# Value pages of paged attention in twelve segments of four or six, instead of sixteen rounds of four

## The chip, the cores and the metric

The kernel runs on one core of one Trainium2 chip. The metric is the device time of one execution in microseconds (us). A core has a matrix engine (TensorE, in the profile PE for matmuls and PEld for the loading of its stationary operand), a vector engine (VectorE, DVE), a scalar engine (ScalarE, ACT), a general engine (GpSimd, POOL) and SyncE (SP), which here only issues DMAs. Each engine runs its own instruction stream in order, and waits on semaphores for the others.

## What is computed

One layer of a decoder runs over 288 tokens: 256 of a prompt, and 32 new ones (8 sequences of 4 tokens) that attend to a paged cache of 1024 earlier rows each. The layer is a feed-forward block, a mixing block, a second feed-forward block, a gated embedding, and a last norm. The change touches one product in the mixing block, the probabilities of the 32 new tokens times the cached values:

```python
def fox_sample(q, k_new, v_new, logf_new, cache_k, cache_v, cache_logf, page_table):
    ...
    v_past = cache_v[page_table].reshape(DB, P, N_HEADS, HEAD_DIM)
    ...
    v_all = jnp.concatenate([v_past.astype(k_new.dtype), v_new], axis=1)
    ...
    p = jax.nn.softmax(s, axis=-1)
    return jnp.einsum('bhqk,bkhd->bqhd', p.astype(v_all.dtype), v_all)
```

There are 8 sequences, 8 pages for each, 128 rows in a page, 8 heads of 128 columns: 64 value pages of 128 x 1024 fp32, 512 KB each. All else in the layer is products of the 288 tokens with weights that are read once.

## The kernel before

**Weight products.** All tokens stand transposed, features on the 128 partitions and 288 tokens along the free axis. A helper, `pair` (L313), makes 256 output features at a time, in chunks of four blocks of 128 input features. For one chunk it needs one weight tile `wraw` of 512 KB, which ScalarE and VectorE split into a high and a low part (`whi`, `wlo`, L294). A chunk is 24 matmuls: for each of 2 output halves and 4 blocks, two with the high weights (L340) and one with the low ones (L342), each streaming 288 columns.

**Order.** The work is a list `steps`. The mixing block's list is written by hand: `fill` is a row of chunks numbered from 0, and `at(i, f)` sets a step `f` ahead of chunk `i`. `between` merges both. A scheduler then lays out every engine's stream, following this order as a priority where the data allow it.

**Loads.** Each step names the items it needs, weights (kind "w") and value pages (kind "p"). `load_upto` (L243) runs ahead of the step by `AHEAD` = 12 items. Weights are issued by SP into four slots in this stage; pages by POOL, as an indirect DMA that gathers 128 rows by index (L261). A page takes one of seven places (`page_tile`, L266): three weight slots that are lent out, three tiles of the pool `vx`, and the tile `wideb`, which holds the scores of the second group of sequences until they have been turned and is first given to page 12. So up to page 11 there are six places. A load can be issued only after the last matmul that read the place's page before.

**The value product.** The 8 sequences are two groups `gi` of four. `probs_t` (L800) turns the probabilities of a group; a sequence's 32 columns (8 heads x 4 tokens) are the stationary operand, 128 x 32, and half a page, 128 x 512, streams past. The matrix engine is cut into four column tiles of 32 columns for it: sequence `b` of the group uses column tile `b`, and its output is 32 rows of a PSUM bank. Two banks `va` hold a group's sums: bank `e` belongs to half `e` of the page's columns (heads 4e to 4e+3). `v_round` (L819) adds page `r` of all four sequences: for e = 0, 1 and b = 0 to 3 one matmul into bank `e`, column tile `b`. Fp32 operands make each a pair of matmul instructions in the trace, so a round has 16. There are 8 rounds for each group, set 2.7 chunks apart (`VSTEP`), ahead of chunks 51, 53, 56, 59, 61, 64, 67, 69 and 72, 75, 78, 80, 82, 86, 88, 91.

**The end of a group.** After its last round `sample_out` (L836) adds the four new tokens (L841, 32 x 32 tiles), picks each row's own head out of the eight blocks with a mask (8 VectorE instructions), and later `sample_turn` (L853) transposes the result (L856) and copies it into `oS` (L858, two copies).

**Other work between the rounds.** Steps `prompt_head` stand 2.5 chunks apart from chunk 69 on. POOL also builds their masks (L878, L879), sums squares (L923, L980) and, from chunk 80 on, adds products to the residual `h` (L1052).

Of the kernel before, what the change touches and what calls it, by code (L numbers as in the profile page):

```python
# [25 lines left out]
P = 128  # L26
# [4 lines left out]
DT = 4  # L31
NS = DB * DT
# [4 lines left out]
PAGES = 8  # L37
# [17 lines left out]
AHEAD = 12  # L55
WARM = (NT, NT, NT)
VSTEP = 2.7

GAINS = ("norm_mix", "norm_ffn2", "norm_ple", "norm_final", "norm_conv_out", "norm_attn_out", "conv_w")
A_ROWS = dict(norm_mix=D, norm_ffn2=D, norm_ple=D, norm_final=D, norm_conv_out=CB * P, norm_attn_out=NH * P,  # L60
# [36 lines left out]
def build(nc, tc, ctx, A, O):  # L97
# [3 lines left out]
    v, s, g, pe, sy = nc.vector, nc.scalar, nc.gpsimd, nc.tensor, nc.sync  # L101
# [13 lines left out]
    def bank(tag, bufs):  # L115
        return ps.tile([P, 512], F32, name=tag, tag=tag, bufs=bufs)
# [6 lines left out]
    def ktbank():  # L123

        names = [n for n in spare["tags"] for _ in range(BANKS[n])]
        spare["at"] += 1
        n = names[spare["at"] % len(names)]
        return bank(n, BANKS[n])
# [6 lines left out]
    def const(name):  # L135
        r, a, b = CONST_COLS[name]
        return C[:r, a:b]
# [7 lines left out]
    at = 0  # L145
# [4 lines left out]
    def gain(name, k):  # L150
        if name == "norm_ffn1":
            return hx[:, k:k + 1]
        a = G[name] + k
        return gT[:, a:a + 1]
# [52 lines left out]
    def split(hi, lo, x, gcol):  # L207
        return (s.activation(hi, x, AF.Copy, scale=gcol),
                v.scalar_tensor_tensor(lo, x, gcol, hi.bitcast(F32), ALU.mult, ALU.subtract))
# [100 lines left out]
    def page(src, j):  # L310
        return dict(kind="p", src=src, rows=idx[:, j:j + 1])
# [65 lines left out]
    def defer(fn, chunks=1):  # L377

        deferred.append((state["chunk"] + chunks, fn))
# [163 lines left out]
    M = {}  # L543
# [256 lines left out]
    def probs_t(gi):  # L800
        pt = wide(*(("vv", "c"), ("mix", "a"))[gi], f"PT{gi}")
        x = M["s", gi]
        for j in range(2):
            t = ktbank()
            for i in range(4):
                c = (4 * j + i) * P
                pe.transpose(t[:, i * P:i * P + P], x[:, c:c + P], ident)
            for b in range(4):
                v.tensor_copy(pt[:, j * 512:j * 512 + 512].rearrange("s (i b c x) -> s b i c x", i=4, b=4, c=4)[:, b],
                              t.rearrange("s (i c b x) -> s b i c x", i=4, c=4, b=4)[:, b])  # L810
        t = ktbank()
        pe.transpose(t[:NS, :P], x[:, PAGES * P:], ident)
        for e in range(2):
            for b in range(4):
                v.tensor_copy(pt[NS * e:NS * e + NS, 8 * P + 32 * b:8 * P + 32 * b + 32].rearrange("s (c x) -> s c x", x=8),
                              t[:NS, :P].rearrange("s (c b x) -> s b c x", c=4, b=4)[:, b])
        M["PT", gi] = pt

    def v_round(gi, r):  # L819
        its = [page(A["cache_v"], (4 * gi + b) * PAGES + r) for b in range(4)]  # L820

        def fn():
            if r == 0:
                M["va", gi] = [bank("va", BANKS["va"]) for _ in range(2)]
                M["pv", gi] = M["PT", gi].rearrange("s (r b x) -> s r b x", b=4, x=32)
            for e in range(2):
                for b in range(4):
                    pe.matmul(M["va", gi][e][32 * b:32 * b + 32, :], M["pv", gi][:, r, b],  # L828
                              its[b]["tile"][:, e * 512:e * 512 + 512], start=r == 0, stop=False, tile_position=(0, 32 * b))
            if r == PAGES - 1:  # L830
                if gi == 1:
                    state.update(through=True, wslot=WEIGHTS - 1)
                sample_out(gi)
        return (its, fn)

    def sample_out(gi):  # L836
        mx = W["vv"][0]
        for b in range(4):
            for e in range(2):
                rows = slice(NS * e, NS * e + NS)  # L840
                pe.matmul(M["va", gi][e][32 * b:32 * b + 32, :], M["pv", gi][rows, 8, b], M["vs"][rows], start=False, stop=True,  # L841
                          tile_position=(NS * e, 32 * b))
        o = mx.tile([P, P], F32, name="so", tag="so", bufs=2)
        for hh in range(NH):
            src = M["va", gi][hh // 4][:, hh % 4 * P:hh % 4 * P + P]
            m = const("headmask")[:, hh:hh + 1]
            if hh == 0:
                v.tensor_scalar(o, src, m, None, ALU.mult)
            else:
                v.scalar_tensor_tensor(o, src, m, o, ALU.mult, ALU.add)  # L850
        defer(lambda: sample_turn(gi, o), 4 if gi == 0 else 2)

    def sample_turn(gi, o):  # L853
        mx = W["vv"][0]
        t = ktbank()
        pe.transpose(t[:, :P], o, ident)  # L856
        for half in range(2):
            v.tensor_copy(M["oS"][:, 4 * half:4 * half + 4, 16 * gi:16 * gi + 16].rearrange("p c (b t) -> p c b t", t=DT),  # L858
                          t[:, :P].rearrange("p (b c a t) -> p a c b t", c=4, a=2, t=DT)[:, half])
        if gi == 1:  # L860
            s.dma_start(O["v_prompt"].rearrange("(j p) c -> p j c", p=P), M["vn"])
            for e in range(2):
                s.dma_start(O["v_sample"][:, 512 * e:512 * e + 512], M["vs"][NS * e:NS * e + NS])
            for hh in range(NH):
                split(za[hh][0][:, SEQ:], za[hh][1][:, SEQ:], M["oS"][:, hh, :], gain("norm_attn_out", hh))
            sq = mx.tile([P, NH, NS], F32, name="sqS")
            s.activation(sq, M["oS"], AF.Square)
            v.tensor_reduce(acc[:, SEQ:], sq.rearrange("p h n -> p n h"), AX.X, ALU.add)
# [173 lines left out]
    def at(i, *fns):  # L1042
        marks.setdefault(i, []).extend(fns)
# [40 lines left out]
    at(48, v_start)  # L1084
    at(50, lambda: probs_t(0))
    at(52, lambda: probs_t(1))
    for r in range(2 * PAGES):
        at({12: 82}.get(r, int(51 + VSTEP * r)), v_round(r // PAGES, r % PAGES))
    for hh in range(NH):
        at(int(69 + 2.5 * hh), lambda hh=hh: prompt_head(hh))  # L1090
    at(80, lambda: norm_scale(rsc, acc2, CB * P, 2))
# [160 lines left out]
```

## Time and profile before

| | |
|---|---|
| median of 3 executions | 2258.11 us |
| lowest and highest | 2255.43, 2260.86 us |
| the profiled execution: its own time | 2257.17 us |
| its span, from the first to the last instruction | 2255.4 us |
| mean granted TensorE clock | 0.998 |
| value rounds (L828) | from 1069.0 us on, the last at 1243.5 us |

The views of this profile are: the page (busy time per engine, the span in 40 slices, DMA queues, the chain of work that ended last, the costliest groups), the timeline (instructions in order of time, alike neighbours merged as "xN"), the instructions of one source line, the waits (who waited for whom), the chain in order of time, and busy times by stretch. All times in them are us from the span's start, unless ns is named. "mm<-x,whi" is an instruction that writes the tile `mm` and reads the tiles `x` and `whi`. A number in square brackets is idle time of that engine just before, and what ended it. A matmul's recorded length is longer than the time until the next one can start, since matmuls are pipelined; what one costs is read from the distance of starts.

### The profile page before, as it was taken

The page shows a single profiled execution, that of the slowest core. Times are in us where ns is not written, and L with a number is a line of the kernel's source. Part 1 is how long each engine was busy: PE and PEld are TensorE (multiplying, and loading weights), DVE is VectorE, ACT ScalarE, POOL GpSimd, SP SyncE. Part 2 cuts the span into 40 slices and gives each one's busy share as a digit, 9 for nine tenths or more (in the row PEclk, how much of TensorE's full clock was granted, in tenths as well). Part 3 has the DMA queues.
Part 4 walks back from the last instruction along what each step waited for, and adds up shares of the span by engine and source line. Part 5 has one row for each costly group of instructions (what it writes and reads, how often), then busy time and mean ns, then how long its engine had stood idle before and what let it go on. Part 6 is the DMA issues. An engine that isn't in the chain of part 4 may idle for free.

```text
span 2255.4 us, 44318 instructions
## 1 busy us (share of the span) xinstructions
PE 2240.5 (99%) x17387; PEld 2184.1 (97%) x17387; DVE 1341.1 (59%) x2413; ACT 1046.4 (46%) x1860; POOL 323.0 (14%) x398
## 2 busy tenths in 40 slices
PE   9999999999999999999999999999999999999997
PEld 9999999999999999888888999999999999999997
DVE  7555555555555586456466875555555555555865
ACT  6444444444444553344344554444444444444654
POOL 1020000000000013344446210000000000000210
PEclk9999999999999999999999999999999999999999
DMA  7575555555555556888988455545555555555552
GB/s 263 170 252 169 170 175 169 171 169 172 173 169 169 169 170 235 335 309 296 330 319 300 171 171 162 182 160 181 174 169 169 172 171 173 168 170 173 170 174 101
DMA packets 342849, 443.37 MB, mean 197 GB/s; under 512 B 17408, under 2 KB 307088, under 8 KB 342640
## 3 DMA queue, kind: packets, MB, share of 16 engines
q1 hardware_dynamic: 320928, 366.25, 49.5%
q0 software_dynamic: 20480, 71.67, 8.8%
q8 instruction: 136, 2.23, 0.4%
q10 hardware_dynamic: 1232, 2.62, 0.3%
q14 instruction: 73, 0.60, 0.1%
HBM read 435.41 MB, written 5.07 MB: 195 GB/s over the span
## 4 chain that ended last, share of the span: by engine, by line
PE 98%; DMA 1%; DVE 0%; issue 0%; ACT 0%; SPq 0%; DVEq 0%; POOL 0%; ACTq 0%
PE mm L340 61%; PE mm L342 31%; PE va L340 1%; PE va L828 1%; PE va L761 1%; PE va L342 1%; DMA KT<-in_cache_k_dram,idx 0%; PE kt L340 0%; DMA page<-in_cache_v_dram,idx 0%; DVE h L1178 0%; DMA h<-in_x_dram 0%; PE kt L342 0%; PE kt L882 0%; PE kt L915 0%; PE kt L906 0%
## 5 line engine op out<-in xcount | busy, mean ns | idle before, releaser
L340 PE MATMUL mm<-x,whi 128*128 128x288 f32 x7360 | 1430.5, 291 | 0.0
L294 DVE TENSOR_TENSOR wlo<-wraw,whi 128x512 fp32r<-128x512 f32 (+1 forms) x1388 | 974.3, 705 | 740.3 <-ACT whi L294 689.5
L294 ACT ACTIVATE whi<-wraw 128x512 fp32r<-128x512 f32 (+1 forms) x1388 | 861.1, 628 | 870.5 <-PE mm L340 755.6
L340 PEld LDWEIGHTS mm<-x,whi 128*128 128x128 f32 x7360 | 1163.4, 187 | 15.9 <-issue 11.0
L342 PE MATMUL mm<-x,wlo 128*128 128x288 f32 x3680 | 1067.4, 290 | 0.1
L342 PEld LDWEIGHTS mm<-x,wlo 128*128 128x128 f32 x3680 | 690.8, 188 | 0.3 <-DVE wlo L294 0.3
L340 PE MATMUL mm<-hid,whi 128*128 128x288 f32 x2816 | 544.8, 290 | 0.0
L340 PEld LDWEIGHTS mm<-hid,whi 128*128 128x128 f32 x2816 | 445.2, 187 | 0.0
L342 PE MATMUL mm<-hid,wlo 128*128 128x288 f32 x1408 | 408.3, 290 | 0.0
L412 POOL TENSOR_TENSOR sr<-sg,rs 128x288 f32<-128x288 f32 x88 | 71.5, 813 | 1385.7 <-ACT sg L410 1385.5
L342 PEld LDWEIGHTS mm<-hid,wlo 128*128 128x128 f32 x1408 | 264.3, 188 | 0.0
L432 DVE SCALAR_TENSOR_TENSOR h<-mm,h 128x288 f32<-128x288 f32 x192 | 85.5, 454 | 19.4 <-PE mm L342 19.4
L410 ACT ACTIVATE sg<-tg 128x288 f32<-128x288 f32 x88 | 39.1, 445 | 97.5 <-DVE tg L408 97.4
L738 POOL DMA_INDIRECT KT<-in_cache_k_dram,idx x64 | 65.2, 1018 | 129.1 <-DVE idx L168 51.6
L419 ACT ACTIVATE hid<-hd 128x288 fp32r<-128x288 f32 x88 | 39.2, 445 | 93.3 <-DVE hd L417 93.3
L261 POOL DMA_INDIRECT page<-in_cache_v_dram,idx x64 | 65.8, 1028 | 66.4 <-PE va L828 43.7
L234 POOL TENSOR_TENSOR acc<-acc,sq 128x288 f32<-128x288 f32 x52 | 43.8, 842 | 219.8 <-ACT sq L233 217.4
L420 DVE TENSOR_TENSOR hid<-hd,hid 128x288 fp32r<-128x288 f32 x88 | 40.1, 457 | 21.9 <-ACT hid L419 21.9
L340 PE MATMUL va<-x,whi 128*128 128x288 f32 x256 | 51.4, 295 | 0.8 <-ACT whi L294 0.8
L340 PE MATMUL mm<-zc,whi 128*128 128x288 f32 x256 | 52.0, 297 | 0.0
L417 DVE TENSOR_TENSOR hd<-mm,sr 128x288 f32<-128x288 f32 x86 | 39.0, 454 | 16.7 <-PE mm L342 16.7
L408 DVE TENSOR_TENSOR tg<-mm,rs 128x288 f32<-128x288 f32 x84 | 37.9, 451 | 14.2 <-PE mm L342 13.1
(236 smaller groups left out, 1060.0 us busy)
## 6 DMA issues: line engine op xcount, KB each, us to landing
wraw<-in_w_ffn_up_dram SPq DMA_DIRECT2D x173, 512.0 KB
wraw<-in_w_ffn_gate_dram SPq DMA_DIRECT2D x172, 512.0 KB
wraw<-in_w_ffn_down_dram SPq DMA_DIRECT2D x160, 512.0 KB
wraw<-in_w_in_dram SPq DMA_DIRECT2D x96, 512.0 KB
wraw<-in_w_out_dram SPq DMA_DIRECT2D x32, 512.0 KB
wraw<-in_w_ple_gate_dram SPq DMA_DIRECT2D x32, 512.0 KB
wraw<-in_w_ffn_down_dram SPq DMA_DIRECT2D x32, 256.0 KB
wraw<-in_w_ple_proj_dram SPq DMA_DIRECT2D x8, 256.0 KB
```

What stands on the lines that cost most here:

```text
L234: (v if k >= KT - last_on_v else g).tensor_tensor(acc, acc, sq, ALU.add)
L261: g.indirect_dma_start(out=t, out_offset=None, in_=it["src"], in_offset=bass.IndirectOffsetOnAxis(ap=it["rows"], axis=0))
L294: for i in s.activation(hi, x, AF.Copy), v.tensor_tensor(lo, x, hi.bitcast(F32), ALU.subtract):
L340: pe.matmul(o, hi[:, j % 2, w], x, start=f, stop=False)
L342: state["product"] = pe.matmul(o, lo[:, j % 2, w], xh, start=False, stop=l)
L410: s.activation(u, t, AF.Silu)
L412: g.tensor_tensor(r, u, rs, ALU.mult)
L417: v.tensor_tensor(t, o, sg[b], ALU.mult)
L419: s.activation(H["hi"][:, k, :], t, AF.Copy)
L420: v.tensor_tensor(H["lo"][:, k, :], t, H["hi"][:, k, :].bitcast(F32), ALU.subtract)
L432: v.scalar_tensor_tensor(h[:, k, :], o, 0.5, h[:, k, :], ALU.mult, ALU.add)
L738: d = g.indirect_dma_start(out=t[:, i].rearrange("p h s -> p (h s)"), out_offset=None, in_=A["cache_k"], in_offset=bass.IndirectOffsetOnAx ...
```

## The change

The list of rounds becomes a list of segments, each given by the pages that it sums. Pages are counted by row first and sequence second, so page number n of a group is row n // 4 of sequence n % 4. A group's 32 pages are cut at `VENDS`: 4, 4, 6, 6, 6, 6 for the first, 6, 6, 6, 6, 4, 4 for the second. A segment stands where the round of its last page would stand by the old rule: ahead of chunks 51, 53, 57, 61, 65, 69 and 73, 78, 82, 86, 88, 91.

In a segment the first four pages are taken as in a round: four matmuls for half 0, four for half 1. Two pages that are left over follow, both for half 0 and then both for half 1. The column tile of half 1 is moved on by two: sequence b uses tile b for half 0 and tile (b + 2) % 4 for half 1. For half 1 of the first four pages, the order of the pages is turned by two, so that the column tiles still come in the same order. `sample_out` uses the same tiles. As the rows of bank 1 now stand two sequences further on, `sample_turn` copies half 1 in two pieces.

The number of matmuls, their shapes, the pages and the weights loaded, the places for pages and `AHEAD` stay as they were.

```diff
+VENDS = ((4, 8, 14, 20, 26, 32), (6, 12, 18, 24, 28, 32))
...
-    def v_round(gi, r):
-        its = [page(A["cache_v"], (4 * gi + b) * PAGES + r) for b in range(4)]
+    def v_round(gi, pages):
+        its = [page(A["cache_v"], (4 * gi + n % 4) * PAGES + n // 4) for n in pages]
...
-            if r == 0:
+            if pages[0] == 0:
...
-            for e in range(2):
-                for b in range(4):
-                    pe.matmul(M["va", gi][e][32 * b:32 * b + 32, :], M["pv", gi][:, r, b],
-                              its[b]["tile"][:, e * 512:e * 512 + 512], start=r == 0, stop=False, tile_position=(0, 32 * b))
-            if r == PAGES - 1:
+            whole = [(i, e) for e in range(2) for i in (range(4) if e == 0 else (2, 3, 0, 1))]
+            for i, e in whole + [(i, e) for e in range(2) for i in range(4, len(pages))]:
+                r, b = divmod(pages[i], 4)
+                c = 32 * ((b + 2 * e) % 4)
+                pe.matmul(M["va", gi][e][c:c + 32, :], M["pv", gi][:, r, b], its[i]["tile"][:, e * 512:e * 512 + 512],
+                          start=r == 0, stop=False, tile_position=(0, c))
+            if pages[-1] == 4 * PAGES - 1:
...
-                pe.matmul(M["va", gi][e][32 * b:32 * b + 32, :], M["pv", gi][rows, 8, b], M["vs"][rows], start=False, stop=True,
-                          tile_position=(NS * e, 32 * b))
+                c = 32 * ((b + 2 * e) % 4)
+                pe.matmul(M["va", gi][e][c:c + 32, :], M["pv", gi][rows, 8, b], M["vs"][rows], start=False, stop=True,
+                          tile_position=(NS * e, c))
...
-        for half in range(2):
-            v.tensor_copy(M["oS"][:, 4 * half:4 * half + 4, 16 * gi:16 * gi + 16].rearrange("p c (b t) -> p c b t", t=DT),
-                          t[:, :P].rearrange("p (b c a t) -> p a c b t", c=4, a=2, t=DT)[:, half])
+        for half, to, at, n in (0, 0, 0, 4), (1, 0, 2, 2), (1, 2, 0, 2):
+            v.tensor_copy(M["oS"][:, 4 * half:4 * half + 4, 16 * gi:16 * gi + 16].rearrange("p c (b t) -> p c b t", t=DT)[:, :, to:to + n],
+                          t[:, :P].rearrange("p (b c a t) -> p a c b t", c=4, a=2, t=DT)[:, half][:, :, at:at + n])
...
-    for r in range(2 * PAGES):
-        at({12: 82}.get(r, int(51 + VSTEP * r)), v_round(r // PAGES, r % PAGES))
+    for gi, ends in enumerate(VENDS):
+        for a, b in zip((0,) + ends, ends):
+            at(int(51 + VSTEP * ((32 * gi + b) / 4 - 1)), v_round(gi, range(a, b)))
```

## The prediction, made before the changed kernel ran

> **What bounds the kernel now.** First the page: busy time, the slices, the chain that ended last.
>
> ```profile
> span 2255.4 us, 44318 instructions
> PE 2240.5 (99%) x17387; PEld 2184.1 (97%) x17387; DVE 1341.1 (59%) x2413; ACT 1046.4 (46%) x1860; POOL 323.0 (14%) x398
> DMA  7575555555555556888988455545555555555552
> PE 98%; DMA 1%; DVE 0%; issue 0%; ACT 0%; SPq 0%; DVEq 0%; POOL 0%; ACTq 0%
> ```
>
> PE is the chain: 98% of it. Whatever the change brings must come out of PE's own stream, or out of a wait of PE. The DMA row says where a wait could come from: in slices 17 to 22 (some 900 to 1240 us) the DMA engines are busy 8 to 9 tenths, elsewhere about 5. The value rounds lie there. The profiled execution took 2257.17 us, 1.8 us more than its span and 0.9 us less than the median of 2258.11; I sum against 2257.17.
>
> Next the timeline of PE around the first round, to price a round.
>
> ```profile
> 1068.74 0.29 PE L342 MATMUL mm<-x,wlo 128*128 128x288 f32 x1
> 1068.96 1.92 PE L828 MATMUL va<-page,PT 128*32 128x512 f32 x16
> 1070.82 0.54 PE L340 MATMUL mm<-x,whi 128*128 128x288 f32 x2
> ...
> 1071.98 0.29 PE L342 MATMUL mm<-x,wlo 128*128 128x288 f32 x1
> ...
> 1073.14 0.29 PE L342 MATMUL mm<-x,wlo 128*128 128x288 f32 x1
> ```
>
> From 1071.98 to 1073.14 nine weight matmuls start, 0.129 us each: the undisturbed pace. From 1068.74 to 1071.98 there are also nine, but it takes 3.24 us. 3.24 - 9 x 0.129 = **2.08 us** is what a round costs PE. How much of it is matmul work shows when a round is cut by the edge of a window:
>
> ```profile
> 1144.04 1.50 PE L828 MATMUL va<-page,PT 128*32 128x512 f32 x12
> ```
>
> ```profile
> 1144.04 1.93 PE L828 MATMUL va<-page,PT 128*32 128x512 f32 x16
> 1145.89 1.09 PE L841 MATMUL va<-vs,PT 32*32 32x512 f32 x16
> 1146.91 0.49 PE L881 MATMUL kt<-k,q 128*128 128x128 f32 x2
> ```
>
> Four more matmuls, one for each column tile, take 0.43 us. They run side by side, since the instructions of one line last this long each:
>
> ```profile
> L828 PE MATMUL va<-page,PT x256: 592/592/617, 1069.0 to 1244.9; 128*32 128x512 f32 x128
> ```
>
> A round of 16 is four such batches, 1.72 us; the other 2.08 - 1.72 = 0.36 us is going into the tiled product and out of it again (0.22 instead of 0.13 us ahead of it, and a slow first pair of weight matmuls behind).
>
> Last, where PE waited. The waits from 1066 to 1250 us and the chain in order of time agree on one place, the third round; the timeline shows its length.
>
> ```profile
> PEld va L828 <- DMA page<-in_cache_v_dram,idx: 1.0, 1, 1.0
> ```
>
> ```profile
> 1082.97 7.76 DMA page<-in_cache_v_dram,idx
> 1090.78 1.90 PE va L828 x10
> ```
>
> ```profile
> 1089.61 3.06 PE L828 MATMUL va<-page,PT 128*32 128x512 f32 x16
> ```
>
> A page issued at 1082.97 landed 7.76 us later; the round took 3.06 instead of 1.92 us, **1.14 us** lost. In all other rounds PE had its pages in time.
>
> **The change part by part.**
>
> *Fewer rounds.* 64 pages are 256 matmuls, 64 batches, before and after: eight segments of six batches and four of four. What goes is four times the way in and out: 4 x 0.36 = **1.45 us**. This holds if the two pages left over fill the array. They come as column tiles b, b+1 for half 0 and b+2, b+3 for half 1: four different tiles, so one batch for each of the two instructions of a product. Two banks are then written side by side. The row of L841 above shows that already: 16 instructions on eight tiles, alternating between the banks, in 1.02 us (1145.89 to 1146.91), about two batches. With two tiles at a time instead, eight segments would pay two batches more each, 8 x 2 x 0.43 = 6.9 us. I take no loss.
>
> *The third round's wait.* The four pages of that round are now first read one chunk later (57 for 56), 24 x 0.129 = 3.1 us, more than the 1.14 us that were short. Two more pages are read in the same segment, 4 batches (1.7 us) behind its start. POOL issues them behind the late one:
>
> ```profile
> 1082.97 0.94 POOL L261 DMA_INDIRECT page<-in_cache_v_dram,idx  x1 [0.30 <-PE mm L342]
> 1084.21 1.41 POOL L261 DMA_INDIRECT page<-in_cache_v_dram,idx  x1 [0.31 <-issue]
> 1085.92 0.94 POOL L261 DMA_INDIRECT page<-in_cache_v_dram,idx  x1 [0.30 <-PE mm L342]
> ```
>
> With 7.76 us again, those land by 1093.7; the segment would start at 1089.6 + 3.2 = 1092.8 and read them from 1094.5. So **-1.14 us**; zero if the pages issued later are slower by more.
>
> *Pages in bursts of five.* There are seven places. With rounds of four, three pages of the next round were there when a round ended. With a segment of six, one page of the next is, and five must be issued once the segment's first four pages are read, 1.85 us after its start T; POOL issues one each 1.25 us:
>
> ```profile
> 1104.94 0.94 POOL L261 DMA_INDIRECT page<-in_cache_v_dram,idx  x1 [6.99 <-PE va L828]
> 1106.19 0.94 POOL L261 DMA_INDIRECT page<-in_cache_v_dram,idx  x1 [0.30 <-issue]
> 1107.43 0.94 POOL L261 DMA_INDIRECT page<-in_cache_v_dram,idx  x1 [0.30 <-PE mm L342]
> 1108.68 0.94 POOL L261 DMA_INDIRECT page<-in_cache_v_dram,idx  x1 [0.30 <-issue]
> ```
>
> The fifth goes out at T + 6.9. With 7.76 us to landing it is there at T + 14.6. The busy times by stretch, cut at the starts of rounds, give the interval:
>
> ```profile
> 1111.71:1123.07 11.36, 11.36 (x90) 9.77 (x89) 4.64 (x9) 3.71 (x7) 4.28 (x4) 1.00 0.97 366
> 1123.07:1135.10 12.03, 12.03 (x95) 10.41 (x95) 5.84 (x12) 3.79 (x7) 4.13 (x4) 1.00 0.89 333
> ```
>
> The first stretch is three chunks and a round: a chunk is (11.36 - 1.85) / 3 = 3.2 us. Four chunks and a segment of six (2.7 us) are 15.4 us, 16.1 with the transposes of the second stretch; the last two pages are read 1.7 us into the next segment, T + 17. That leaves 2.5 us. The first stretch also shows DMA share 0.97 at 366 GB/s, so a fifth page in a row may need longer than 7.76 us; no row has such a burst. Bounds: nothing, or 1.5 us in each of the four intervals between chunks 57 and 73; I take 0.5 us in all, near the nothing that 2.5 us of room give.
>
> The Trainium skill, in "DMA: Bandwidth & Descriptors", section on the anatomy of a DMA on the GpSimd path, fits such a load as 2.0 us and its bytes at 436 GB/s; for 512 KB that is an estimate of 3.2 us, by which neither this term nor the next would exist and the sum would be -2.6 us. The trace has 7.76 us, and I go by the trace.
>
> *The pair of segments at 86 and 88.* Two chunks apart, with six pages ahead of four: only one of the four is there, three must be issued, where before one was. POOL's timeline there:
>
> ```profile
> 1222.77 2.38 POOL L1052 TENSOR_TENSOR h<-h,tB 128x288 f32<-128x288 f32 x2 [1.00 <-DVE tB L1051]
> 1225.30 0.95 POOL L261 DMA_INDIRECT page<-in_cache_v_dram,idx  x1 [0.15 <-issue]
> 1226.56 0.94 POOL L261 DMA_INDIRECT page<-in_cache_v_dram,idx  x1 [0.30 <-PE mm L340]
> 1227.80 1.11 POOL L261 DMA_INDIRECT page<-in_cache_v_dram,idx  x1 [0.31 <-PE mm L342]
> ```
>
> ```profile
> 1221.24 1.93 PE L828 MATMUL va<-page,PT 128*32 128x512 f32 x16
> ```
>
> ```profile
> 1231.15 1.92 PE L828 MATMUL va<-page,PT 128*32 128x512 f32 x16
> ```
>
> The interval is 9.91 us and becomes 10.8 with two batches more. The page issued at 1225.30 landed within 5.85 us, as PE did not wait for it at 1231.15. The third page goes out at T + 4.4 if POOL turns to the pages at once, at 1227.80 - 1221.24 = T + 6.6 behind the two adds, and lands 5.85 to 7.76 us later: T + 10.2 to T + 14.3, against 10.8. PE loses 0 to 3.5 us; I take **1.4 us**, POOL going to the pages after one of the adds. Behind PE's wait stand only weight matmuls; their weights are loaded meanwhile.
>
> *Small parts.* Two more copies of `oS` on DVE, off the chain:
>
> ```profile
> L858 DVE COPY oS<-kt x4: 212/214/224, 1161.9 to 1251.7; 128x64 f32<-128x64 f32 x4
> ```
>
> DVE is 59% busy, so they cost nothing; without cover 0.4 us. L841 keeps eight different tiles: nothing, within one batch (0.43 us) either way for each group.
>
> **The sum:** -1.45 - 1.14 + 0.5 + 1.4 = -0.7 us. 2257.17 - 0.7 = **2256.5 us**. By the bounds: from -2.6 to -1.45 + 6 + 3.5 = +8 us.
>
> **Rivals.**
>
> *Late pages, slower.* The mechanism of the bursts, at its upper end: every segment of six that follows another by four chunks starts 2 us short, because 5 pages and the weights share DMA engines that stand at 0.97. Six such intervals (chunks 57 to 73 and 78 to 86) and 3 us at 88: 15 us, less 2.6: about 2269.6; with half the waits 2262. It decides from some 10 us to landing for the fifth page. For it: 7.76 us for a third page in a row. Against: the mean rate, 10 tiles of 0.52 MB in 15.4 us, 340 GB/s, is below the 366 that a stretch moved.
>
> The Trainium skill, in "SBUF — State Buffer", section "SBUF: two separate sides", says that POOL cannot write a DMA's descriptors while VectorE holds the port they share. That would stretch bursts. The trace bears it out little: issues of L261 last 936 ns at least, 942 in the median, 2020 at most.
>
> *Left-over pages do not share the array* (the change fails to do what it says): -1.45 + 6.9 - 1.14 + 1.9 gives 2263.4. Against it stands the row of L841.
>
> *Nothing gained:* the way in and out costs a longer segment more, or the waits are worth what the rounds were: 2257 to 2258.
>
> *More gained:* no wait anywhere, 2254.6, and a favourable draw of executions.
>
> **How the numbers follow.** A measurement of this kernel can tell some 0.2%, 4.5 us. Forecast (2254.5 to 2258.5) 0.65; nothing gained 0.10; late pages 0.17; array not shared 0.03; more gained 0.05. Executions of the kernel before ranged over 5.4 us, so the range is wider than the bounds of the forecast: 2252.5 to 2263. Faster by over 0.2% needs more than the whole saving, only spread can show it: 0.07. Slower: late pages and unshared array, less their milder half, 0.16. Within: 0.77.
>
> **What would show it.** Twelve groups of L828, of 24 matmuls in about 2.78 us or of 16 in 1.92. If a group of 24 takes near 4.5 us without a DMA wait, the array is not shared. Waits of PEld at L828 for page DMAs: one of 1 to 2 us at the segment of chunk 88, none at the third segment. If such waits sum to more than 6 us, the bursts decide and the forecast is wrong. If DVE or ACT end waits of PE, the scheduler has moved other work, which I left out.

## The result: slower by 0.3%, and the profile after

| | before | changed |
|---|---|---|
| median of 7 executions, us | 2256.78 | 2264.86 |
| lowest and highest, us | 2255.43, 2260.86 | 2261.20, 2266.16 |
| the profiled execution, us | 2257.17 | 2261.20 |
| its span, us | 2255.4 | 2259.4 |

The ratio changed / before is 1.003, with a 95% interval of 1.0021 to 1.004. The changed kernel is slower, by 8 us in the medians. Its profiled execution happens to be its fastest one; a second trace, from a usual execution, comes with the experiments.

The page of the changed kernel reads almost as before: the span and the chain that ended last. The lines have moved by one to four: L831 is now the value product, L262 the page load, L341 and L343 the weight products.

```profile
span 2259.4 us, 44310 instructions
PE 98%; DVE 1%; DMA 1%; issue 0%; POOL 0%; ACT 0%; DVEq 0%; ACTq 0%; POOLq 0%
```

DVE has come up to 1%. Where the time went shows in the chain in order of time, from 1060 to 1262 us, here without its PE pieces for weights:

```profile
1067.96 1.95 PE va L831 x16
1070.08 1.04 POOL page L262
1071.43 0.98 POOL page L262
1072.71 7.39 DMA page<-in_cache_v_dram,idx
1080.15 1.90 PE va L831 x10
1095.32 2.71 PE va L831 x24
...
1195.73 0.99 DVE zc L210
...
1228.53 6.64 DMA page<-in_cache_v_dram,idx
1235.21 1.91 PE va L831 x12
```

Two page loads that PE waited for now stand on the chain, where the kernel before had one, and a stretch of DVE's work lies on the chain near 1195 us. The timeline of PE gives the lengths. The second segment (chunk 53, four pages, as before) and the one at chunk 88 (four pages):

```profile
1077.15 1.40 PE L831 MATMUL va<-page,PT 128*32 128x512 f32 x6
1080.15 1.90 PE L831 MATMUL va<-page,PT 128*32 128x512 f32 x10 [1.60 <-DMA page<-in_cache_v_dram,idx]
...
1231.59 1.04 PE L831 MATMUL va<-page,PT 128*32 128x512 f32 x2
1233.94 1.05 PE L831 MATMUL va<-page,PT 128*32 128x512 f32 x2 [1.30 <-DMA page<-in_cache_v_dram,idx]
1235.21 1.91 PE L831 MATMUL va<-page,PT 128*32 128x512 f32 x12 [0.23 <-DMA page<-in_cache_v_dram,idx]
```

The first lasts 1080.15 + 1.90 - 1077.15 = 4.90 us instead of 1.92: **3.0 us** lost at chunk 53. The other lasts 1235.21 + 1.91 - 1231.59 = 5.53: **3.6 us** lost at chunk 88. Each time some of the matmuls run, and the rest stand until a page lands.

The third segment, which in the old place waited for 1.14 us, does not wait, and a segment of six looks like this:

```profile
1095.25 2.78 PE L831 MATMUL va<-page,PT 128*32 128x512 f32 x24
```

2.78 - 1.92 = 0.86 us more than four pages, two batches, so the two left-over pages do share the array. Eight such additions are 6.9 us, four rounds less at 2.06 us (the same reading of the first round, 1068.74 to 1071.19 less three weight matmuls) are 8.2 us: **1.4 us** saved.

The last piece is at the norm of the conv group, ahead of the output projection. PE's timeline there, after and then before:

```profile
1200.52 0.40 PE L192 MATMUL kt<-sqh,meanr 128*128 128x288 f32 x1
1201.27 0.40 PE L192 MATMUL kt<-sql,meanr 128*128 128x288 f32 x1 [0.35 <-DVE sql L205]
```

```profile
1202.45 0.38 PE L191 MATMUL kt<-sqh,meanr 128*128 128x288 f32 x1
1202.67 0.29 PE L191 MATMUL kt<-sql,meanr 128*128 128x288 f32 x1
```

The second matmul comes 0.75 instead of 0.22 us behind the first: PE has reached it before VectorE has made `sql`. With a second such wait of 0.3 us in the product before (for `zc`, the last rows of the conv group), and what each adds around it, PE loses **1.1 us** that the kernel before did not lose.

The account of this execution: -1.4 - 1.1 + 3.0 + 3.6 + 1.1 = +5.2 us. The spans differ by 4.0, since the first segment of this execution also began 1.1 us earlier (1067.9 against 1069.0 us), with the same program ahead of it: the spread of executions.

### The profile page after: what moved, and what is told of

It reads as the page before. It is cut to its first block, busy times and chain, and to the rows that moved or that the text cites. A ratio compares the mean times of both kernels' runs of the same rounds, so it can differ in the third digit from the quotient of the medians.

```text
span 2259.4 us, 44310 instructions
## 1 busy us (share of the span) xinstructions
PE 2242.1 (99%) x17387; PEld 2184.8 (97%) x17387; DVE 1344.8 (60%) x2415; ACT 1047.1 (46%) x1860; POOL 321.2 (14%) x398
## 3 DMA queue, kind: packets, MB, share of 16 engines
q8 instruction: 136, 2.23, 0.4%
## 4 chain that ended last, share of the span: by engine, by line
PE 98%; DVE 1%; DMA 1%; issue 0%; POOL 0%; ACT 0%; DVEq 0%; ACTq 0%; POOLq 0%
PE mm L341 61%; PE mm L343 30%; PE va L341 2%; PE va L831 1%; PE va L762 1%; PE va L343 1%; DMA page<-in_cache_v_dram,idx 1%; PE kt L341 0%; DVE h L1183 0%; PE kt L343 0%; PE mm L521 0%; PE kt L886 0%; PE kt L919 0%; DVE wlo L295 0%; PE kt L910 0%
## 5 line engine op out<-in xcount | busy, mean ns | idle before, releaser
L341 PE MATMUL mm<-x,whi 128*128 128x288 f32 x7360 | 1430.0, 291 | 0.0
L341 PEld LDWEIGHTS mm<-x,whi 128*128 128x128 f32 x7360 | 1163.4, 187 | 13.3 <-issue 11.8
L343 PE MATMUL mm<-x,wlo 128*128 128x288 f32 x3680 | 1067.3, 290 | 0.1
L343 PEld LDWEIGHTS mm<-x,wlo 128*128 128x128 f32 x3680 | 690.7, 188 | 0.3 <-DVE wlo L295 0.3
L341 PE MATMUL mm<-hid,whi 128*128 128x288 f32 x2816 | 544.8, 290 | 0.0
L341 PEld LDWEIGHTS mm<-hid,whi 128*128 128x128 f32 x2816 | 445.1, 187 | 0.0
L343 PE MATMUL mm<-hid,wlo 128*128 128x288 f32 x1408 | 408.3, 290 | 0.0
L343 PEld LDWEIGHTS mm<-hid,wlo 128*128 128x128 f32 x1408 | 264.3, 188 | 0.0
L262 POOL DMA_INDIRECT page<-in_cache_v_dram,idx x64 | 64.3, 1005 | 72.9 <-PE va L831 49.4
L341 PE MATMUL mm<-zc,whi 128*128 128x288 f32 x256 | 52.0, 297 | 0.1
L341 PE MATMUL va<-x,whi 128*128 128x288 f32 x256 | 51.4, 295 | 0.0
```

What stands on the lines that cost most here:

```text
L262: g.indirect_dma_start(out=t, out_offset=None, in_=it["src"], in_offset=bass.IndirectOffsetOnAxis(ap=it["rows"], axis=0))
L341: pe.matmul(o, hi[:, j % 2, w], x, start=f, stop=False)
L343: state["product"] = pe.matmul(o, lo[:, j % 2, w], xh, start=False, stop=l)
```

## The experiments

Two questions were open: why does a segment wait whose four pages, places and chunk are as before, and why are the three pages at chunk 88 so late? Four kernels were run together; the kernel before had a median of 2256.94 us beside them.

**Release order.** The trace names, for each wait of PE, the semaphore of the load it waits for. In the kernel before, the second round waits for the first and second load of POOL's burst after the first round; in the changed kernel for the second and third, and the third segment waits for the first. By these waits POOL has put page 8 ahead of pages 6 and 7. Page 8 takes the place of page 2, and the turned order (2, 3, 0, 1) of the second half reads page 2 for the last time first. So the theory: the turn lets go of the wrong place first. The edit takes only the turn out:

```diff
-            whole = [(i, e) for e in range(2) for i in (range(4) if e == 0 else (2, 3, 0, 1))]
+            whole = [(i, e) for e in range(2) for i in range(4)]
```

> The changed kernel, with the first four pages of a segment taken in the order 0, 1, 2, 3 for both halves (the turn by two taken out; column tiles and segments as changed). Theory A (release order): the turned order lets go of the third page's place first, so that POOL issues page 8 ahead of pages 6 and 7, and the segment at chunk 53 waits for page 7; here the order of issue is 6, 7, 8 again, the wait of some 3 us at the second segment is under 0.5 us, and the time is about 3 us under the changed kernel's, 2259 to 2262 us; the wait at chunk 88 stays at some 3.6 us, since all three late pages are needed at once in whatever order they come. Theory B (chance): pages 4 to 7 and their places are as before, the wait at chunk 53 is the luck of one execution; no gain, 2263 to 2266 us. The matmuls themselves should cost the same, 2.94 us for a segment of six, or up to 0.9 us more for each segment if the order of column tiles matters.

Measured: 2260.70 us (2258.41 to 2263.46), ratio to the kernel before 1.0018 [1.0009, 1.0027]; 4.2 us under the changed kernel's median. The burst, in POOL's timeline, went out at the same distances, and the second segment did not wait (PE's timeline, second fence):

```profile
1071.53 1.04 POOL L262 DMA_INDIRECT page<-in_cache_v_dram,idx  x1 [4.29 <-PE va L831]
1072.88 0.98 POOL L262 DMA_INDIRECT page<-in_cache_v_dram,idx  x1 [0.30 <-issue]
1074.17 0.94 POOL L262 DMA_INDIRECT page<-in_cache_v_dram,idx  x1 [0.30 <-PE mm L343]
```

```profile
1078.59 1.92 PE L831 MATMUL va<-page,PT 128*32 128x512 f32 x16
1109.70 3.73 PE L831 MATMUL va<-page,PT 128*32 128x512 f32 x24
1231.00 1.92 PE L831 MATMUL va<-page,PT 128*32 128x512 f32 x6
1234.59 1.90 PE L831 MATMUL va<-page,PT 128*32 128x512 f32 x10 [1.68 <-DMA page<-in_cache_v_dram,idx]
```

The segment at 1078.59 waits for the first and second load again. Chunk 88 still loses 1234.59 + 1.90 - 1231.00 - 1.92 = 3.6 us. The matmuls cost the same in the natural order. One wait is new here: 3.73 - 2.78 = 0.95 us at chunk 61, the burst of five that the prediction feared.

**The turn alone.** The same question from the other side: rounds of four at the old chunks, with the moved column tiles and the turn.

```diff
-VENDS = ((4, 8, 14, 20, 26, 32), (6, 12, 18, 24, 28, 32))
+VENDS = (range(4, 33, 4), range(4, 33, 4))
...
-        for a, b in zip((0,) + ends, ends):
-            at(int(51 + VSTEP * ((32 * gi + b) / 4 - 1)), v_round(gi, range(a, b)))
+        for a, b in zip((0,) + tuple(ends), ends):
+            at({52: 82}.get(32 * gi + b, int(51 + VSTEP * ((32 * gi + b) / 4 - 1))), v_round(gi, range(a, b)))
```

> Sixteen rounds of four at the chunks of the kernel before, but with the moved column tiles and the turned order of the second half. Theory A (release order): the turn alone moves page 8 ahead of pages 6 and 7, so a wait of 1 to 3 us shows at the second round, and 1.1 us or less stays at the third: 1 to 3 us over the kernel before. Theory B (chance, or the segments): equal to the kernel before within 1 us. A round costs PE 2.08 us in both.

Measured: 2260.74 us (2259.48 to 2263.24), ratio 1.0015 [1.0006, 1.0024]: 3.8 us lost with not one segment of six. The second round, in PE's timeline:

```profile
1079.08 1.06 PE L831 MATMUL va<-page,PT 128*32 128x512 f32 x6
1082.83 3.51 PE L831 MATMUL va<-page,PT 128*32 128x512 f32 x10 [2.69 <-DMA page<-in_cache_v_dram,idx]
```

It lost 1082.83 + 3.51 - 1079.08 - 1.92 = 5.3 us, more than expected, and the third round lost nothing. Not all of the 5.3 us is waiting: the ten matmuls behind the wait took 3.51 us instead of 1.90, and the busy times by stretch show why. PEclk, the granted clock of TensorE (the third number from the end), is 0.50 there:

```profile
1083.00:1086.40 3.40, 3.40 (x11) 0.48 (x3) 0.00 (x0) 0.00 (x0) 1.18 (x2) 0.50 0.54 219
```

So 5.3 - 1.6 = 3.7 us are the wait. The last section comes back to the clock. Both sides agree: the wait at chunk 53 comes from the turn, by way of POOL's order of loads. All five traces with the turn have it, with 1.4 to 3.7 us; the seven without the turn lose 0.13 us there at most. Why its size differs so much is not shown.

**Room at chunk 88.** The segment is set one chunk later, all else as changed:

```diff
-            at(int(51 + VSTEP * ((32 * gi + b) / 4 - 1)), v_round(gi, range(a, b)))
+            at({60: 89}.get(32 * gi + b, int(51 + VSTEP * ((32 * gi + b) / 4 - 1))), v_round(gi, range(a, b)))
```

> The changed kernel, with the segment of chunk 88 (pages 24 to 27 of the second group) at chunk 89. Theory of the burst: three pages have to be issued and to land between the segments at 86 and 88, and come 3.6 us late; one chunk later is 3.2 us more room, so the wait there falls to about 0.5 us and the time by about 3 us, to 2260 to 2263 us; the wait at chunk 53 stays. Rival: the pages at 88 are late because the DMA engines or POOL have no room at all there, so the wait moves with the segment, and the time stays at 2263 to 2266 us.

Measured: 2258.77 us (2257.89 to 2263.01), ratio 1.001 [1.0001, 1.0019]; 6.1 us under the changed kernel, more than the 3 expected. Of these its trace shows 3.1: from the start of the first segment to the start of the last it is 176.6 us, for 179.7 in the first trace of the changed kernel. PE's timeline shows 2.23 - 1.92 = 0.3 us left at the moved segment, and the wait at chunk 53 still there (3.2 us):

```profile
1077.71 1.06 PE L831 MATMUL va<-page,PT 128*32 128x512 f32 x6
1080.91 1.90 PE L831 MATMUL va<-page,PT 128*32 128x512 f32 x10 [2.14 <-DMA page<-in_cache_v_dram,idx]
...
1235.78 2.23 PE L831 MATMUL va<-page,PT 128*32 128x512 f32 x16
```

**Both edits together.**

> The changed kernel with both edits: pages 0, 1, 2, 3 in order for both halves, and the segment of chunk 88 at chunk 89. If release order and the burst at 88 are the whole cause, only the savings stay: 4 x 0.36 us of switching and the 1.1 us wait of the third round, 2 to 3 us under the kernel before. If other waits are behind the changed kernel's 8 us in the median (its profiled execution, with 4 us, was its fastest), the time stays above the kernel before.

Measured: 2256.41 us (2254.58 to 2258.22), ratio 0.9998 [0.9989, 1.0007]. The 8 us are gone, but of the 2 to 3 us that should have been left over, 0.5 shows in the medians; in its trace the stretch from the first segment to the last is 1.3 us shorter than before. No wait for a page is left in its trace over 0.2 us. The waits of PE from 1065 to 1262 us name what remains:

```profile
PEld kt L192 <- DVE sql L205: 0.6, 1, 0.6
PEld mm L341 <- DVE zc L210: 0.3, 1, 0.3
```

The single effects (4.2 and 6.1 us) add up to more than both together (8.4); the traces account for the terms of single executions, not for that.

**A second trace of the changed kernel**, since the first was of its fastest execution. This and the next three were run together, beside a median of 2257.25 us before.

> The changed kernel once more, for a second trace of it. Its first trace was its fastest execution (2261.20 us, 3.7 us under its median) and had two waits for pages, 3.0 us at chunk 53 and 3.6 us at chunk 88. If page loads are the whole cause, a usual execution has the same two waits, longer: together some 9 to 11 us, in a time of 2263 to 2266 us. If something else costs the rest, the two waits are as long as in the first trace and another wait stands beside them.

Measured: 2263.93 us (2262.43 to 2269.71), ratio 1.0038 [1.0024, 1.0052]; the profiled execution took 2263.93 us. PE's timeline at chunks 53 and 88, and the waits of PE:

```profile
1078.82 1.14 PE L831 MATMUL va<-page,PT 128*32 128x512 f32 x6
1080.24 1.90 PE L831 MATMUL va<-page,PT 128*32 128x512 f32 x10 [0.28 <-DMA page<-in_cache_v_dram,idx]
...
1234.49 1.05 PE L831 MATMUL va<-page,PT 128*32 128x512 f32 x2
1236.48 1.04 PE L831 MATMUL va<-page,PT 128*32 128x512 f32 x2 [0.95 <-DMA page<-in_cache_v_dram,idx]
1237.93 1.91 PE L831 MATMUL va<-page,PT 128*32 128x512 f32 x12 [0.40 <-DMA page<-in_cache_v_dram,idx]
```

```profile
PEld mm L341 <- DVE zc L210: 1.8, 1, 1.8
PEld kt L681 <- DVE tB L691: 1.2, 3, 0.6
...
PEld kt L192 <- DVE sql L205: 0.6, 1, 0.6
```

The page waits are 1.4 and 3.4 us, less than in the first trace. The expectation that they would be longer was wrong; the other reading holds in part. The span is 2.7 us longer than that of the first trace. 1.7 us of this lie ahead of the first segment (1069.56 against 1067.89 us), with the same program. From the first segment to the last it is 1.1 us longer, though the page waits are 1.8 us less. What grew there is VectorE: 1.8 + 1.2 + 0.6 = 3.6 us of such waits, on PE's queue of weight loads, against 0.9 in the first trace. None of these three lines stands in the waits of the kernel before.

**What VectorE's waits hang on.** The kernel before had a round at chunk 80, just ahead of the first conv products of the output projection. While it ran, VectorE worked on the rows of `zc` (one of two such instructions took from 1195.96 to 1196.95 us, the round from 1194.92 to 1196.84). The changed kernel has segments at 78 and 82. First try: move the waiting matmul instead, one chunk on.

```diff
-    at(80, lambda: norm_scale(rsc, acc2, CB * P, 2))
+    at(80, lambda: norm_scale(rsc, acc2, CB * P, 3))
```

> The version with both edits (order 0 to 3 for both halves, the last but one segment at chunk 89), and the matmul of the conv group's norm one chunk later (deferred by 3 chunks instead of 2). In the version with both edits PE loses 1.1 us there that the kernel before does not lose: it meets that matmul ahead of VectorE, with no round at chunk 80 in front of it. If that is so, the trace shows those 1.1 us gone and the time 2255 to 2256 us, 1 to 2 us under the kernel before. Rival: VectorE is then late for the first evacuation of the output projection, which needs the norm's factor, and the loss only moves.

Measured: 2261.84 us (2260.02 to 2264.89), ratio 1.0019 [1.001, 1.0028], some 5 us worse than without it (5.4 in the medians, 5.1 when each is set against the kernel before that ran beside it). The wait for `sql` is gone, and PE waits for `zc` (2.3 us) and for a prompt head's probabilities instead:

```profile
PEld mm L341 <- DVE zc L210: 2.3, 1, 2.3
PEld kt L919 <- ACT pT L912: 2.2, 1, 2.2
```

The loss moved and grew, as the rival had it, but not to the evacuation that the rival named. PE itself stood for 2.0 and 1.8 us in these two waits. Behind each of them the granted clock was 0.50 for 3.4 us, which is another 1.7 us of work each time. The two waits and the slow clock, 7.2 us, are about what this stretch of the trace has more than that of the version with both edits (181 against 173 us). Why VectorE and ScalarE are so late here is not shown.

**POOL's adds at chunk 88.**

```diff
             v.tensor_tensor(t, o, rsc, ALU.mult)
-            g.tensor_tensor(h[:, k, :], h[:, k, :], t, ALU.add)
+            v.tensor_tensor(h[:, k, :], h[:, k, :], t, ALU.add)
```

> The changed kernel, with the residual adds of the conv part of the output projection on VectorE instead of POOL. If the wait at chunk 88 comes from POOL doing two adds (2.4 us) ahead of the three late page loads, it falls from 3.6 us and more to some 1.2 us, and the time to some 2.4 us under the changed kernel's 2264.9 us. If the loads are late for their own landing time alone, the wait and the time stay. The wait at chunk 53 stays in either case.

Measured: 2263.30 us (2260.78 to 2264.13), ratio 1.0026 [1.0016, 1.0036]. The segment at chunk 88 now lasts 2.61 us, a wait of 0.7 instead of 3.4 to 3.6. POOL's timeline of the changed kernel and of this one show why:

```profile
1223.11 2.40 POOL L1056 TENSOR_TENSOR h<-h,tB 128x288 f32<-128x288 f32 x2 [0.99 <-DVE tB L1055]
1226.03 0.95 POOL L262 DMA_INDIRECT page<-in_cache_v_dram,idx  x1 [0.52 <-issue]
```

```profile
1229.40 0.95 POOL L262 DMA_INDIRECT page<-in_cache_v_dram,idx  x1 [4.72 <-PE va L831]
```

```profile
1237.20 2.61 PE L831 MATMUL va<-page,PT 128*32 128x512 f32 x16
```

The segments at chunk 86 began at 1220.81 and 1226.42 us. The first load went out 5.2 us after that in the one and 3.0 us in the other. So POOL's adds do make up most of that wait. A gain in time is not shown: the median is 0.6 us under that of the changed kernel in the same set of executions (2263.93) and 1.6 us under its first one, both less than the executions differ, and not 2.4 or more. VectorE carries the adds now, and PE waits for it 1.8 us at `zc` and 1.7 us at `tB` (L691); the granted clock also fell to 0.50 for 3.4 us once. The waits at `zc` and `tB` are about as long in the second trace of the changed kernel, so they are not shown to come from the adds.

**The shift of column tiles**, taken out of the version with both edits (`c = 32 * b` for both halves, and the copies in `sample_turn` to match):

> The version with both edits, without the shift of column tiles: a page's second half uses the column tile of the first, as in the kernel before. The two pages left over in a segment then have two column tiles for four matmuls. By the reading that column tiles work side by side and each in its own order, a segment of six costs two batches more, 0.86 us, eight times 6.9 us: 2263 us, and a group of 24 matmuls lasts 3.6 us instead of 2.8. If the array does not care which tiles come next to each other, the time stays at 2256.4 us.

Measured: 2264.06 us (2263.19 to 2266.84), ratio 1.0032 [1.0021, 1.0043]; 7.7 us over the version with both edits (7.3 when each is set against the kernel before that ran beside it). A segment of six, in PE's timeline:

```profile
1093.75 3.63 PE L831 MATMUL va<-page,PT 128*32 128x512 f32 x24
```

3.63 - 2.78 = 0.85 us more, eight times 6.8 us. So in these segments the column tile that the next matmul uses decides what runs side by side.

**A segment at chunk 80 again.** The second group is cut otherwise, with the natural order; this and the next ran beside a median of 2256.84 us before.

```diff
-VENDS = ((4, 8, 14, 20, 26, 32), (6, 12, 18, 24, 28, 32))
+VENDS = ((4, 8, 14, 20, 26, 32), (6, 10, 16, 22, 28, 32))
```

> The changed kernel with pages 0, 1, 2, 3 in order for both halves, and the second group cut at 6, 10, 16, 22, 28, 32: segments ahead of chunks 73, 76, 80, 84, 88, 91, so that one stands at chunk 80 again and no two are nearer than three chunks. Theory of the cover: where the kernel before had a round at chunk 80, VectorE gets 1.9 us to finish the last conv rows ahead of the first product that reads them; the changed kernel has no segment there and loses 1 to 2.5 us between chunks 80 and 82 (1.1 us in the version with both edits, where page waits are gone). Here that loss is gone as well: all savings stay, 2 to 2.6 us under the kernel before, 2254 to 2255.5 us, with no wait of PE over 0.5 us for pages, zc or sql. Rival: segments that stand elsewhere leave VectorE late at some other place, and the time stays at 2256 to 2257 us.

Measured: 2255.50 us (2254.43 to 2259.46), ratio 0.9995 [0.9985, 1.0004]. Of PE's waits for `zc`, `sql` and `tB` (L691) none is left. What is left are page waits of 0.7 us in two pieces, and a new wait of PE for VectorE, 0.5 us at `tB` of the output projection (L1055), which is the rival in small. It is the lowest median of all versions, 1.3 us under the kernel before, but the interval includes 1: a gain is not shown.

**The kernel before, its round of chunk 80 at 79.**

```diff
-        at({12: 82}.get(r, int(51 + VSTEP * r)), v_round(r // PAGES, r % PAGES))
+        at({11: 79, 12: 82}.get(r, int(51 + VSTEP * r)), v_round(r // PAGES, r % PAGES))
```

> The kernel before, with only its round of chunk 80 moved to chunk 79. Theory of the cover: PE then waits for VectorE at the first conv product of the output projection and at the norm's matmul, 1 to 2.5 us together, and some 0.3 us for a page at the moved round; 2258 to 2260 us. If those waits belong to the segments and not to the place of the round, the time stays within 0.7 us of the kernel before.

Measured: 2259.38 us (2257.20 to 2260.97), ratio 1.0011 [1.0002, 1.002]. The waits of PE:

```profile
PEld va L828 <- DMA page<-in_cache_v_dram,idx: 3.2, 3, 1.6
...
PEld kt L191 <- DVE sql L204: 0.8, 1, 0.8
```

The wait for `sql` appears in the kernel before as soon as its round leaves chunk 80; a wait for `zc` does not. Most of the 2.5 us is page waits (1.7 us at the moved round, where 0.3 was expected), since the moved round is only one chunk behind the one before it. So the place of the round covers the norm's matmul, and the run with a segment at 80 shows the same from the other side. All twelve traces fit: the three with a round or segment at chunk 80 (the kernel before, the turn alone, this last cut) have no wait for `sql` and none for `zc`; the other nine have one for `sql`, or, where that matmul was moved, a longer one for `zc`. Why VectorE is late for `zc` and at the transposes (L681) in some executions and not in others is not settled.

## Why the prediction was wrong

*Bound by PE; loss only as a wait of PE.* Right. In both traces of the changed kernel all of the loss is PE waiting inside the stretch of the value product; that a wait can also be followed by a slower clock was not thought of.

*Fewer rounds, -1.45 us.* Right: 1.4 us, by 0.86 us for two batches more. That left-over pages share the array was right; the run without the shift shows 6.8 us for the 6.9 that were named as its price.

*The third round's wait, -1.14 us.* Right: it is gone at chunk 57.

*Pages in bursts of five, +0.5 us.* Its low bound came: nothing in both traces of the changed kernel; 0.95 us once, in the run with the natural order.

*The segments at 86 and 88, +1.4 us.* The place and the mechanism were right, the term was mis-sized: 3.4 and 3.6 us, the upper bound of 3.5. Both of POOL's adds went ahead of the loads, where one had been taken, and the three loads then followed in a row: the last went out at 1228.53, T + 7.7 for the T + 6.6 of the upper end, and landed 6.64 us later.

*What failed: the second segment was not priced at all.* The prediction reads "in all other rounds PE had its pages in time" as if that were room. The second round had none: it took 1.96 us instead of 1.92 in the kernel before, so its last page landed as it started.

```profile
1078.22 1.96 PE L828 MATMUL va<-page,PT 128*32 128x512 f32 x16
```

The change leaves that segment's pages and chunk alone, but the turned order of the second half changes which place comes free first. The prediction did not follow the turn to the places it frees and to POOL's queue behind them. This cost 3.0 us in the first trace and 1.4 in the second, and 3.8 us in the medians when tried alone.

*What was missing besides: the work that the removed rounds covered.* Four ways in and out were counted as saved. A round at chunk 80 also gave VectorE time. Losing that time cost PE 1.1 us in the first trace. In the second the stretch of the value product grew by 6.2 us, and -1.4 - 1.1 + 1.4 + 3.4 leave 3.9 us; VectorE's waits are all that the trace names for them, and those at L681 do not belong to chunk 80. "DVE or ACT end waits of PE" stood in the prediction only as something that would make it wrong, with no price.

*The rival "late pages"* named the mechanism that decided, pages that PE waits for, and looked for most of it, 12 of 15 us, where segments of six follow each other by four chunks. Those had room. It came where the room was smallest before: two chunks apart, where the rival had 3 us, and the tight first burst. The bounds of the sum, up to +8 us, reach 2265.2 us and so take in the median, but with 6 us for bursts that cost nothing; that is luck, and the stated range ended at 2263.

On the Trainium skill, "DMA: Bandwidth & Descriptors", section on the anatomy of a DMA on the GpSimd path: its fit would be an estimate of 3.2 us for a page, by which the wait at chunk 53 would not exist and the one at chunk 88 would be 0.1 us. The loads that ended the waits took 7.39 and 6.64 us. The measurement decides.

## What to carry to other kernels

When a change alters the order in which buffers are read for the last time, follow it to the queue that refills them: the scheduler issues loads in the order in which places come free, and a load put one step back can cost more than the whole change saves. A consumer that does not wait has an unknown amount of room; before moving or merging steps, read from the trace how long after its issue each load is needed, and price the tightest one. A piece of work that is taken off the bounding engine also takes away the time that it gave to the engines beside it.

## What the runs showed of the hardware that was not expected

**Column tiles.** In a segment that waits for a page, matmuls of the other column tiles run on: six matmuls at 1077.15 us ran while the fourth page was missing, the second instruction of three products ahead of the first instruction of the fourth. In a segment that does not wait, the first instructions of all four products come first; cut by a window that ends at 1203.3 us, the segment at 1203.16 us shows four that start within 0.05 us, of 0.59 us each:

```profile
1203.16 0.64 PE L831 MATMUL va<-page,PT 128*32 128x512 f32 x4
```

The program is the same for both, so it alone does not fix the order in which matmuls of different column tiles start. An order in which column tiles do not come strictly in turn (the natural order with the moved tiles) cost nothing measurable: segments of 2.78 us in the run with a segment at 80 as in the changed kernel.

```profile
1192.80 2.78 PE L831 MATMUL va<-page,PT 128*32 128x512 f32 x24
```

**The clock after a wait.** In three traces the granted clock of TensorE falls to 0.50 for 3.4 us between 1060 and 1262 us: once with the turn alone (from 1083.0 us), twice with the norm's matmul moved (from 1201.8 and 1215.4 us), once with the adds on VectorE (from 1205.8 us). It begins 0.2 to 2.1 us after the end of a wait in which PE stood for 1.6 to 2.7 us, and costs about 1.7 us each time, which no wait shows. What sets it off is open: five waits of PE of 1.6 to 2.1 us, in the traces of the changed kernel among others, were not followed by it. The seven executions of the changed kernel fit it: the three with a mean granted clock of 0.998 took 2261.20 to 2263.37 us, the four with 0.997 took 2264.86 to 2266.16 us. Of those four there is no trace, so that such falls make up part of the 8 us is likely but not shown.
